# Moving two small tiles so that TensorE's two operands start a multiple of 512 bytes apart

## The chip, the cores and the metric

The kernel runs on one core of a Trainium2 chip. The metric is device time in microseconds of one execution, the median of several. The engines are named as the profile names them: PE is TensorE (its matmuls), PEld is TensorE's load of the stationary operand, DVE is VectorE, ACT is ScalarE, POOL is GpSimd, SP is SyncE, whose queue issues the weight transfers.

## The reference

One decoder block on 256 tokens of width 2048, all in float32. What is computed, cut to its matrix products:

```
x = x + 0.5 * swiglu(rmsnorm(x), w_gate, w_up, w_down)         # hidden width 5632
h = rmsnorm(x);  proj = h @ w_in                               # 2048 x 11264
y_a = diff_attention(dq, dk, dv);  y_b = hgrn2(hq, hf, hi, hg) # 8 heads each
merged = sigmoid(gate_a) * (y_a @ w_branch_a) + sigmoid(gate_b) * (y_b @ w_branch_b)
x = x + merged @ w_out
x = x + 0.5 * swiglu(rmsnorm(x), w_gate2, w_up2, w_down2)
x = x + sigmoid(rmsnorm(x) @ w_ple_gate) * rmsnorm(p @ w_ple_proj)
```

## The kernel before

All large products go through one stream of weights. A **group** is two blocks of 128 rows by 512 columns of a weight matrix. `prep` brings it from HBM into `raw` (SP's queue), rounds it to `wh` (ACT, line 114) and puts the remainder into `wl` (DVE, line 115), three groups ahead of use. `group` (lines 148 to 150) then multiplies: for each of the two blocks and each of the two halves of the tokens (`tt`) there are three matmuls, high activation by `wh`, high by `wl`, low by `wh`, so 12 matmuls in a group. The activation is the **stationary** operand, 128 by 128, loaded anew for every matmul; the weight is the **moving** operand, 128 by 512.

The activations stand in pairs of tiles, high and low part: `AH`, `AL` for the products of the normed block input (gate and up, `w_in`, `w_ple_gate`), `hH`, `hL` for the down products, `yaH`, `yaL` and `ybH`, `ybL` for the two branches, `mH`, `mL` for `w_out`, `pH`, `pL` for `w_ple_proj`. Of the 512-column matmuls 6672 load `AH` or `AL`, 2112 `hH` or `hL`, 384 `mH` or `mL`, 192 `ybH` or `ybL`, 192 `yaH` or `yaL`, 48 `pH` or `pL`.

The order of the work is written out by hand. Between two groups, `advance` lets each running task issue its next piece (transposes through PE, attention, the recurrence, residuals). A run of large matmuls is thus cut where a task puts small matmuls on PE: in the gate and up stage four transposes of `h` (line 209) after each 96 large matmuls, in the down stage four transposes of `x` at two places 12 matmuls apart in each chunk of 264, in the mixing stage at many places.

Where tiles stand: a pool lays its tags one behind the other, each buffer rounded up to 32 bytes, and a pool opened later stands behind those still open. Every weight buffer, `wh` and `wl` alike, starts 64 bytes above a multiple of 512. Inside the tiles a matmul's operand starts a multiple of 512 bytes from the tile's start (`AH[:, kt, tcol(tt)]` at 1024 kt + 512 tt, `wh[:, k2, :]` at 2048 k2). So the distance of the two operands, modulo 512, is that of the tiles:

```
tile         start (bytes in the partition)  start mod 512   minus that of wh, wl
wh, wl        93248 and on, steps of 4096         64              0
AH            34816                                0            -64
AL            51200                                0            -64
hH           126016                               64              0
hL           171072                               64              0
yaH, yaL     150592, 158784                       64              0
pH, pL       136256, 138304                       64              0
ybH, ybL     175200, 183392                       96            +32
mH, mL       191584, 207968                       96            +32
```

`AH` and `AL` follow `x` in the pool `base`; `ss4`, two buffers of 32 bytes, follows them. `gsub`, one number per partition (line 335), stands in the pool `mid` behind `yaL`, takes 32 bytes there, and so pushes all that the later pools put behind it, `ybH`, `ybL`, `mH` and `mL` among them, by 32 bytes.

## Time and profile before

| | |
|---|---|
| median of 3 runs | 2322.2 us (2322.05 to 2322.46) |
| profiled execution, first to last instruction | 2320.3 us |
| PE busy | 2312.7 us |
| DVE busy | 1270.9 us |
| ACT busy | 1042.7 us |
| HBM traffic | 186 GB/s over the span |

The profiled execution is told by its span alone; the median of the runs is 1.9 us longer, which is taken as what lies around the span. A matmul's row in the trace lasts longer than the step from one matmul to the next, since matmuls are pipelined: a row of 0.39 us stands beside a step of about 0.23 us. So the time that a matmul takes of the span is read from the starts of successive matmuls, not from its duration.

### The profile page before, as it was taken

How to read it: one execution, taken by the hardware profiler on the slowest of the kernel's cores; microseconds unless marked ns; L12 is line 12 of the kernel's file. 1: busy time of each engine (PE TensorE's matmuls, PEld its weight loads, DVE VectorE, ACT ScalarE, POOL GpSimd, SP SyncE). 2: the span in 40 equal slices, each digit the busy share in tenths (PEclk: the TensorE clock that was granted, in tenths of full speed). 3: DMA queues.
4: the chain of work that ended last, by engine and by line, in shares of the span. 5: the costliest groups of instructions: out<-in, count | busy, mean ns of one | idle time of the engine just before them, and what ended most of it. 6: DMA issues, size and time to landing. Idle time of an engine off the chain costs nothing.

```text
span 2320.3 us, 27206 instructions
## 1 busy us (share of the span) xinstructions
PE 2312.7 (100%) x10564; PEld 1903.2 (82%) x10564; DVE 1270.9 (55%) x1381; ACT 1042.7 (45%) x1270; POOL 39.5 (2%) x38
## 2 busy tenths in 40 slices
PE   9999999999999999999999999999999999999999
PEld 7888888888888888888888888888888888888887
DVE  5554555554444576667765555555555554444456
ACT  6444444444444455543344444544444444444454
POOL 0000000000000100000010000000000000000000
PEclk9999999999999999999999999999999999999999
DMA  8655555566666645554455655565555556666664
GB/s 292 190 182 191 190 188 185 189 189 188 188 188 196 201 161 167 186 173 153 160 156 181 186 186 181 179 193 184 189 190 185 188 188 190 193 188 191 188 213 149
DMA packets 120464, 432.55 MB, mean 186 GB/s; under 512 B 13773, under 2 KB 14181, under 8 KB 120208
## 3 DMA queue, kind: packets, MB, share of 16 engines
q1 hardware_dynamic: 118800, 426.33, 58.3%
q0 software_dynamic: 1248, 4.43, 0.5%
q8 instruction: 82, 1.34, 0.2%
q14 instruction: 46, 0.38, 0.0%
q10 hardware_dynamic: 288, 0.07, 0.0%
HBM read 428.67 MB, written 2.11 MB: 186 GB/s over the span
## 4 chain that ended last, share of the span: by engine, by line
PE 99%; DMA 1%; DVE 0%; ACT 0%; SPq 0%; issue 0%; ACTq 0%; DVEq 0%
PE acc L148 32%; PE acc L150 31%; PE acc L149 31%; PE tp L209 1%; PE ms L616 1%; DMA raw<-in_gu 0%; PE tp L219 0%; PE ms L440 0%; PE ms L150 0%; PE ms L149 0%; PE ms L148 0%; PE ms L589 0%; PE tp L362 0%; DMA junk<-in_xT 0%; PE tp L477 0%; PE ms L641 0%
## 5 line engine op out<-in xcount | busy, mean ns | idle before, releaser
L115 DVE TENSOR_TENSOR wl<-raw,wh 128x1024 fp32r<-128x1024 f32 (+1 forms) x805 | 983.9, 1223 | 888.9 <-ACT wh L114 886.5
L114 ACT CAST wh<-raw 128x1024 fp32r<-128x1024 f32 (+1 forms) x805 | 844.9, 1051 | 941.1 <-PE acc L150 915.6
L148 PE MATMUL acc<-wh,AH 128*128 128x512 f32 x2224 | 885.2, 398 | 0.2 <-ACT wh L114 0.2
L150 PE MATMUL acc<-wh,AL 128*128 128x512 f32 x2224 | 872.3, 392 | 0.0
L149 PE MATMUL acc<-wl,AH 128*128 128x512 f32 x2224 | 866.9, 390 | 1.6 <-DVE wl L115 1.6
L150 PEld LDWEIGHTS acc<-wh,AL 128*128 128x128 f32 x2224 | 417.7, 188 | 95.5
L149 PEld LDWEIGHTS acc<-wl,AH 128*128 128x128 f32 x2224 | 418.1, 188 | 91.5 <-DVE wl L115 3.7
L148 PEld LDWEIGHTS acc<-wh,AH 128*128 128x128 f32 x2224 | 418.4, 188 | 84.7 <-ACT wh L114 1.7
L148 PE MATMUL acc<-wh,hH 128*128 128x512 f32 x704 | 275.3, 391 | 0.0
L150 PE MATMUL acc<-wh,hL 128*128 128x512 f32 x704 | 274.2, 390 | 0.0
L149 PE MATMUL acc<-wl,hH 128*128 128x512 f32 x704 | 273.9, 389 | 0.0
L150 PEld LDWEIGHTS acc<-wh,hL 128*128 128x128 f32 x704 | 132.1, 188 | 27.8
L149 PEld LDWEIGHTS acc<-wl,hH 128*128 128x128 f32 x704 | 132.2, 188 | 27.1
L148 PEld LDWEIGHTS acc<-wh,hH 128*128 128x128 f32 x704 | 132.2, 188 | 27.1
L263 ACT ACTIVATE s<-acc,rowr 128x256 f32<-128x256 f32 x86 | 40.8, 477 | 49.9 <-PE acc L150 49.9
L183 ACT CAST hH<-tp 128x512 fp32r<-128x512 f32 x44 | 25.8, 587 | 74.7 <-PE tp L209 74.7
L184 DVE TENSOR_TENSOR hL<-tp,hH 128x512 fp32r<-128x512 f32 x44 | 30.4, 692 | 46.6 <-ACT hH L183 46.5
L265 DVE SCALAR_TENSOR_TENSOR h<-acc,rowr,s 128x256 f32<-128x256 f32 x86 | 41.4, 483 | 20.6 <-ACT s L263 20.6
L148 PE MATMUL acc<-wh,mH 128*128 128x512 f32 x128 | 51.3, 401 | 0.0
L149 PE MATMUL acc<-wl,mH 128*128 128x512 f32 x128 | 50.6, 395 | 0.0
L150 PE MATMUL acc<-wh,mL 128*128 128x512 f32 x128 | 50.6, 395 | 0.0
L186 ACT ACTIVATE AH<-tp,gains 128x256 fp32r<-128x256 f32 x48 | 22.9, 477 | 31.0 <-PE tp L209 16.9
(191 smaller groups left out, 1019.9 us busy)
## 6 DMA issues: line engine op xcount, KB each, us to landing
raw<-in_gu SPq DMA_DIRECT2D x351, 512.0 KB, 3.5
raw<-in_down SPq DMA_DIRECT2D x176, 512.0 KB, 3.8
raw<-in_w_in SPq DMA_DIRECT2D x176, 512.0 KB, 3.6
raw<-in_w_out SPq DMA_DIRECT2D x32, 512.0 KB, 3.7
raw<-in_w_pg SPq DMA_DIRECT2D x32, 512.0 KB, 4.3
raw<-in_w_a SPq DMA_DIRECT2D x16, 512.0 KB, 3.5
raw<-in_w_b SPq DMA_DIRECT2D x16, 512.0 KB, 3.5
junk<-in_xT SPq DMA_DIRECT2D x8, 256.0 KB, 4.2
```

The source lines that it names most:

```text
L114: nc.scalar.copy(wh[:, ks, :], raw[:, ks, :])
L115: nc.vector.tensor_tensor(wl[:, ks, :], raw[:, ks, :], wh[:, ks, :].bitcast(F32), op=ALU.subtract)
L148: nc.tensor.matmul(dst, hi, wh[:, k2, cols], start=(kt == 0), stop=False)
L149: nc.tensor.matmul(dst, hi, wl[:, k2, cols], start=False, stop=False)
L150: nc.tensor.matmul(dst, lo, wh[:, k2, cols], start=False, stop=(kt == last))
L183: nc.scalar.copy(H, src)
L184: nc.vector.tensor_tensor(L, src, H.bitcast(F32), op=ALU.subtract)
L186: nc.scalar.activation(H, src, AF.Copy, scale=gain)
L209: nc.tensor.transpose(tp[:, i, tcol(tt)], src_of(tt, kt + i), ident)
L263: nc.scalar.activation(s, acc[tt][:, :HALF], AF.Silu, scale=rs[0][:, tt : tt + 1])
L265: nc.vector.scalar_tensor_tensor(h[tt], acc[tt][:, HALF:], rs[0][:, tt : tt + 1], s, op0=ALU.mult, op1=ALU.mult)
L616: nc.tensor.matmul(lp[:, i, tt, :], km[:, i, tt, :], q4[:, i, tt, :], start=True, stop=True)
```

## The change

Three small edits move tiles. `gsub` becomes the fifth column of the tile of `small` in the pool `base`, whose 16 bytes grow to 20 within the same 32. `ss4` is allocated ahead of `AH` and `AL` instead of behind them. No instruction is added, removed or moved on any engine, and the waits stand as they did; the one instruction that writes `gsub`, and those that read it, name another tile. Comments taken out of the file are left out here.

```
-    small = T(base, [P, 4], "small")
+    smalls = T(base, [P, 5], "small")
+    small, gsub = smalls[:, 0:4], smalls[:, 4:5]
     ident = T(base, [P, P], "ident")
     x = T(base, [P, NT, D], "x")
+    ss4 = new_ss4()
     act = new_act()
-    ss4 = new_ss4()
...
     yaH = T(mp, [P, NH, SEQ], "yaH", F32R)
     yaL = T(mp, [P, NH, SEQ], "yaL", F32R)
-    gsub = T(mp, [P, 1], "gsub")
     nc.vector.tensor_scalar(gsub, small[:, S_SUB : S_SUB + 1], 1.0 - LAMBDA_INIT, None, op0=ALU.mult)
```

After it `AH` starts at 34880 and `AL` at 51264 (64 above a multiple of 512), `ybH` and `ybL` at 175168 and 183360, `mH` and `mL` at 191552 and 207936 (64 above as well). `wh`, `wl`, `hH`, `hL`, `yaH`, `yaL`, `pH` and `pL` stay. So all tiles of the table have a distance of 0 modulo 512 from the weights. Other tiles of the attention, the recurrence and the merge move 32 bytes down; the operands of their small matmuls keep their distance, but for the products with `V`, whose `A` and `off` move while `V` stays, and the transposes of `tok`, `ya` and `SG` against `ident`, which stays.

## Rows read from the trace of the kernel before

**Rows 1.** The page: span, PE's busy time, granted clock by slice, chain that ended last.

```profile
span 2320.3 us, 27206 instructions
...
PE 2312.7 (100%) x10564; PEld 1903.2 (82%) x10564; DVE 1270.9 (55%) x1381; ACT 1042.7 (45%) x1270; POOL 39.5 (2%) x38
...
PEclk9999999999999999999999999999999999999999
...
PE 99%; DMA 1%; DVE 0%; ACT 0%; SPq 0%; issue 0%; ACTq 0%; DVEq 0%
```

**Rows 2.** What PE waited for: total us, times, longest.

```profile
PE acc L149 <- DVE wl L115: 1.6, 3, 0.8
PE ms L290 <- DVE warm L287: 1.2, 1, 1.2
```

**Rows 3.** The longest wait of all engines, the same columns.

```profile
ACT wh L114 <- PE acc L150: 915.6, 554, 3.5
```

**Rows 4.** PE's groups by line: out<-moving,stationary, count, busy us, mean ns.

```profile
L149 PE MATMUL acc<-wl,AH 128*128 128x512 f32 x2224 | 866.9, 390 | 1.6 <-DVE wl L115 1.6
L149 PE MATMUL acc<-wl,hH 128*128 128x512 f32 x704 | 273.9, 389 | 0.0
L149 PE MATMUL acc<-wl,mH 128*128 128x512 f32 x128 | 50.6, 395 | 0.0
L209 PE MATMUL tp<-ident,h 128*128 128x128 f32 x176 | 26.3, 271 | 0.0
L209 PE MATMUL tp<-ident,x 128*128 128x128 f32 x96 | 14.4, 272 | 0.0
L149 PE MATMUL acc<-wl,pH 128*128 128x512 f32 x16 | 6.2, 389 | 0.0
```

**Rows 5.** Timeline (start, duration us): a run of 96 on `AH`, `AL` between transposes.

```profile
281.74 0.48 PE L148 MATMUL acc<-wh,AH 128*128 128x512 f32 x1
282.05 0.40 PE L149 MATMUL acc<-wl,AH 128*128 128x512 f32 x1
...
303.58 0.39 PE L150 MATMUL acc<-wh,AL 128*128 128x512 f32 x1
```

**Rows 6.** Timeline: the run of 48 on `ybH`, `ybL`, first and last.

```profile
1272.27 0.40 PE L148 MATMUL acc<-wh,ybH 128*128 128x512 f32 x1
...
1283.24 0.40 PE L150 MATMUL acc<-wh,ybL 128*128 128x512 f32 x1
```

**Rows 7.** Timeline: a run of 84 on `mH`, `mL` behind transposes.

```profile
1415.41 0.48 PE L148 MATMUL acc<-wh,mH 128*128 128x512 f32 x1
1415.72 0.40 PE L149 MATMUL acc<-wl,mH 128*128 128x512 f32 x1
...
1434.86 0.39 PE L150 MATMUL acc<-wh,mL 128*128 128x512 f32 x1
```

**Rows 8.** Timeline: `hH`, `hL`, 264 from 506.00, then 12 from 566.34.

```profile
506.00 0.48 PE L148 MATMUL acc<-wh,hH 128*128 128x512 f32 x1
...
534.01 0.39 PE L148 MATMUL acc<-wh,hH 128*128 128x512 f32 x1
...
565.75 0.40 PE L150 MATMUL acc<-wh,hL 128*128 128x512 f32 x1
...
566.34 0.48 PE L148 MATMUL acc<-wh,hH 128*128 128x512 f32 x1
...
568.97 0.40 PE L150 MATMUL acc<-wh,hL 128*128 128x512 f32 x1
```

**Rows 9.** Timeline: `pH`, `pL`, the second and the last of a run of 24.

```profile
2238.65 0.40 PE L149 MATMUL acc<-wl,pH 128*128 128x512 f32 x1
...
2243.64 0.39 PE L150 MATMUL acc<-wh,pL 128*128 128x512 f32 x1
```

**Rows 10.** Timeline: `yaH`, `yaL`, first and last of 24 behind products with `V`.

```profile
1200.30 0.48 PE L148 MATMUL acc<-wh,yaH 128*128 128x512 f32 x1
...
1205.61 0.39 PE L150 MATMUL acc<-wh,yaL 128*128 128x512 f32 x1
```

## The prediction, made before the result was known

> **What bounds the kernel now.** I read the page first, then PE's waits, then PE's groups, then the timeline inside single stages. [...] PE waits 2.8 us in the whole span [rows 2], while the longest wait of all is that of ACT for PE, 915.6 us, because ACT may not overwrite a weight buffer that PE still reads [rows 3]. So the only thing that can move the end is the step from one large matmul to the next, and any change of that step reaches the end undiminished: ACT and DVE have slack in every group, and the transfers are issued three groups ahead.

> The step itself is not the same everywhere. The durations of the rows in the groups only hint at it (389 and 390 ns on `AH`, `hH` and `pH`, 395 ns on `mH`) [rows 4]; it must be taken from starts. On `AH`, `AL` the 95 matmuls from 282.05 to 303.58 make 94 steps in 21.53 us, 229.0 ns each [rows 5]. On `ybH` 47 steps take 10.97 us, 233.4 ns [rows 6]; on `mH` the 82 steps from 1415.72 take 19.14 us, 233.4 ns [rows 7]. On `hH` the last 140 steps of a run, 534.01 to 565.75, take 31.74 us, 226.7 ns [rows 8]; on `pH` 22 steps take 4.99 us, 226.8 ns [rows 9]. These are the same instructions, 128 by 128 stationary and 128 by 512 moving, with moving tiles from the same `wh` and `wl`. Set beside the table of places they fall into three classes: distance 0 modulo 512 gives 226.7 ns, distance -64 gives 229.0, distance +32 gives 233.4. The stage isn't the cause: `pH` runs between products on `AH`, and `ybH` between products on `AH` too, with the same side work around them. Nor is the part of memory: `hL` covers 171072 to 216128, which holds `ybH` and most of `mH`, and runs at the fast step. Inside a tile the step doesn't change from one token half to the other, though these stand 512 bytes apart, so what counts repeats within 512 bytes.

> **The change part by part.** No instruction, wait or transfer is added, removed or moved, so nothing has to be hidden; `gsub` is still written once by DVE, off the chain. What changes is the distance: 0 for `AH`, `ybH` and `mH` and their low parts.

> First, the steady step. 6672 matmuls on `AH`, `AL` (2224 on each of three lines) [rows 4] go from 229.0 to 226.7: 6672 x 2.3 = 15.3 us. 192 on `ybH`, `ybL` go from 233.4 to 226.7: 1.3 us. 384 on `mH`, `mL` the same: 2.6 us. Sum 19.2 us. The 96 half-wide matmuls at the end on `AH` have no row at distance 0; at most the same 2.3 ns each, 0.2 us, left out. The 2352 matmuls already at distance 0 gain nothing.

> Second, the restart, which works against the change. After small matmuls on PE the steady step isn't there at once. On `AH` a run from 281.74 to 303.58 has 95 steps in 21.84 us; at 229.0 they would take 21.76, so the restart costs 0.09 us over the steady step [rows 5]. On `hH` the 11 steps from 566.34 to 568.97 take 2.63 us and would take 2.49 at 226.7: 0.14 us [rows 8]. The run from 506.00 to 565.75, which follows transposes of `h` as the runs on `AH` do, has 263 steps in 59.75 us against 59.62: 0.13 us [rows 8]. On `yaH`, behind products with `V`, 23 steps take 5.31 us against 5.21: 0.10 us [rows 10]. So the aligned pair settles later, and a restart costs 0.01 to 0.05 us more than on `AH`. The program has 118 restarts on `AH`: 42 behind four transposes of `h` (176 transposes are 44 blocks, two of them ahead of `hH`) [rows 4], 42 behind other transposes, 34 behind small products. At 0.04, 0.05 and 0.01 us more: 1.7 + 2.1 + 0.3 = 4.1 us. On `mH` there are 8; the 83 steps from 1415.41 take 19.45 us against 19.37, 0.08 us for the restart [rows 7], so 0.06 more each: 0.5 us. Sum 4.6 us.

> Net 19.2 - 4.6 = 14.6 us. Against the profiled execution: span 2320.3 - 14.6 = 2305.7 us; with the 1.9 us around it, 2307.6.

> Bounds. Best: the restart on `AH` gets no dearer (one run alone stands for restarts behind transposes of `h`): gain 19.2, time 2303. Worst within the mechanism: every restart on `AH` costs what the dearest row shows, 0.14 us instead of 0.09, and those on `mH` the 0.06 more (5.9 + 0.5 us), and `AH` settles 0.4 ns above 226.7 (2.7 us; an estimate from the 0.01 us to which the rows are rounded, on 22 steps): gain 10.1, time 2312. The small matmuls whose distance changes (products with `V`, transposes against `ident`) have nothing at another distance that is alike; transposes of `x` and `h` stand at distances 0 and 64 from `ident` and their groups' means are 272 and 271 ns [rows 4], so some 200 of them are 0.2 us either way.

> The next bound after PE is far: a group of 12 takes 2.72 us instead of 2.75, and ACT still waits for PE for hundreds of us [rows 3]. PE's 2.8 us of waits [rows 2] may grow by what PE gains ahead of its first weights, 0.2 us.

> [...]

> **The rivals.**

> The second operand's place isn't what slows `AH`; only `ybH` and `mH` gain. For it: `AH` and `AL` stand lowest of all, partly below 65536, where no fast tile stands, and -64 is a different case from +32. Against it: the high and low tiles of the down products lie spread over 88 KB and run at one step, so place alone has shown no effect but by the distance. Gain 1.3 + 2.6 - 0.5 = 3.4 us: 2318.8.

> Distance has no effect at all, as if each tile carried its step with it by some other property (who wrote it, and when). For it: each kind of tile has its own writer. Against it: `ybH` and `yaH` are made by the same function (`branch_input`), and 23 steps on `yaH` with a restart among them take 5.31 us, 230.9 ns each, less than the 233.4 of `ybH` without one [rows 6, 10]. Time 2322.2.

> Slower: the aligned pair fails to settle. The place is the gate and up stage, 44 runs of about 96 matmuls behind transposes. On `hH` a restart costs 0.05 us more than on `AH`, spread over 11 steps [rows 8]: some 231.3 ns each beside what both pay, above the 229.0 of `AH`; if the runs of 96 stayed there, 4224 matmuls would lose 2.3 ns each, 9.7 us, and the mixing stage's runs of 12 to 36 (2112 matmuls) as much each, 4.9 us, against 3.4 gained on `ybH` and `mH`: 2322.2 + 11 = 2333. It decides when settling takes longer than the gain of a run pays for: 0.04 to 0.05 us more a restart against 2.3 ns a step, so 17 to 22 matmuls. Against it: the last 140 steps of a run on `hH` stand at 226.7 [rows 8]. Runs of 12 are on the wrong side of that point already, and their loss is in the sum.

> **How the numbers follow.** The mechanism as summed: 0.83, its own range 2303 to 2312. Only `ybH` and `mH`: 0.06. No effect: 0.05. Slower: 0.06. I predict 2307.6. For 8 in 10 the range must hold nearly all of the first case, so it goes a little beyond its bounds, 2302 to 2313, where a second unknown adds to the first. The runs of before agree within 0.4 us of each other; 0.2%, 4.6 us, is about what a measurement can tell from no change. The first case is faster (below 2317.6), the second and third are the same, the fourth is slower: 0.83, 0.11, 0.06.

> **What would show it.** The steady step on `AH`, `mH` and `ybH` at 226.7 ns in the timeline, and that on `hH`, `yaH` and `pH` unchanged. The first ten or so steps behind transposes in the gate and up stage above 226.7, making some 0.13 us a restart instead of 0.09. One chunk of that stage, 96 large matmuls and four transposes, some 0.18 us shorter than now. PE's waits still below 4 us, and ACT's for PE a little shorter. The prediction is wrong if the step on `AH` stays at 229.0 (then a place below 65536 or the tile itself is the cause), if it settles at a fourth value, or if the runs of 96 never settle.

## The result and the profile after

The changed kernel takes 2307.17 us (median of 4 runs, 2306.70 to 2307.39) against 2322.26 us of before: 15.1 us less, a ratio of 0.9935 with a 95% interval of 0.9923 to 0.9947. The forecast was 2307.6. The profiled executions differ by a little more, 2320.3 to 2304.2 us; the spans of the four runs after go from 2304.2 to 2305.3, so about 1 us of the 16.1 is play between executions.

The page of the changed kernel, lines as in [rows 1]:

```profile
span 2304.2 us, 27206 instructions
...
PE 2296.5 (100%) x10564; PEld 1903.1 (83%) x10564; DVE 1270.9 (55%) x1381; ACT 1041.0 (45%) x1270; POOL 39.4 (2%) x38
...
PE 98%; DMA 1%; DVE 0%; ACT 0%; SPq 0%; issue 0%; ACTq 0%
```

The whole gain is on PE: its busy time falls by 16.2 us, while DVE's stays and ACT's falls by 1.7 us. The waits of the changed kernel, total us, times and longest, as in [rows 2, 3]:

```profile
PE ms L290 <- DVE warm L287: 1.2, 1, 1.2
PE acc L149 <- DVE wl L115: 1.0, 2, 0.8
PE acc L148 <- ACT wh L114: 0.5, 1, 0.5
...
ACT wh L114 <- PE acc L150: 904.6, 554, 3.5
```

PE waits 2.7 us in all, 0.1 less than before, and ACT waits 11 us less for PE: PE was the bound and still is. The step was read as ahead, from the starts of large matmuls in the changed kernel's timeline (start, duration in us):

```profile
277.96 0.48 PE L148 MATMUL acc<-wh,AH 128*128 128x512 f32 x1
278.28 0.39 PE L149 MATMUL acc<-wl,AH 128*128 128x512 f32 x1
...
299.60 0.39 PE L150 MATMUL acc<-wh,AL 128*128 128x512 f32 x1
...
300.18 0.48 PE L148 MATMUL acc<-wh,AH 128*128 128x512 f32 x1
...
321.85 0.39 PE L150 MATMUL acc<-wh,AL 128*128 128x512 f32 x1
...
322.43 0.48 PE L148 MATMUL acc<-wh,AH 128*128 128x512 f32 x1
...
560.63 0.48 PE L148 MATMUL acc<-wh,hH 128*128 128x512 f32 x1
...
563.26 0.40 PE L150 MATMUL acc<-wh,hL 128*128 128x512 f32 x1
...
1264.60 0.39 PE L148 MATMUL acc<-wh,ybH 128*128 128x512 f32 x1
...
1275.25 0.39 PE L150 MATMUL acc<-wh,ybL 128*128 128x512 f32 x1
...
1405.28 0.48 PE L148 MATMUL acc<-wh,mH 128*128 128x512 f32 x1
...
1424.23 0.40 PE L150 MATMUL acc<-wh,mL 128*128 128x512 f32 x1
```

The run of 48 on `ybH` makes 47 steps in 10.65 us, 226.6 ns each, where it had 233.4 [rows 6]. A run of 96 on `AH` makes its 95 steps in 21.64 us, the next in 21.67, where one took 21.84 [rows 5]; at 226.7 ns they would take 21.54, so the restart behind transposes now costs 0.10 us in one chunk and 0.13 in the next, by turns. The 83 steps on `mH` take 18.95 us instead of 19.45 [rows 7], 0.13 over 18.82. The restart on `hH` is what it was, 2.63 us for 11 steps [rows 8]. One chunk of the gate and up stage, from the first large matmul to that of the next, lasts 22.22 and 22.25 us by turns, where it lasted 22.43 (326.59 to 349.02): 0.21 and 0.18 us less, with a forecast of some 0.18.

### The profile page after: what moved, and what is told of

It is laid out like the page before. It is cut to its first block, busy times and chain, and to the rows that moved or that the text cites. A ratio compares the mean times of both kernels' runs of the same rounds, so it can differ in the third digit from the quotient of the medians.

```text
span 2304.2 us, 27206 instructions
## 1 busy us (share of the span) xinstructions
PE 2296.5 (100%) x10564; PEld 1903.1 (83%) x10564; DVE 1270.9 (55%) x1381; ACT 1041.0 (45%) x1270; POOL 39.4 (2%) x38
## 4 chain that ended last, share of the span: by engine, by line
PE 98%; DMA 1%; DVE 0%; ACT 0%; SPq 0%; issue 0%; ACTq 0%
PE acc L148 31%; PE acc L150 31%; PE acc L149 31%; PE tp L209 1%; PE ms L616 1%; DMA raw<-in_gu 1%; PE tp L219 0%; PE ms L440 0%; PE ms L149 0%; PE ms L150 0%; PE ms L148 0%; PE ms L589 0%; PE tp L362 0%; ACT wh L114 0%; PE tp L477 0%
```

## The experiments

In all tables a step is worked out from two starts in the timeline of one run of large matmuls, past its first 12 where a restart lies ahead of it, divided by the steps between. The kernel before, run beside each group of experiments, took 2321.7 to 2322.5 us (medians).

**The two parts alone.** `e1` moves `ss4` only, `e2` moves `gsub` only.

```
 e1:                                   e2:
-    act = new_act()                   -    small = T(base, [P, 4], "small")
     ss4 = new_ss4()                   +    smalls = T(base, [P, 5], "small")
+    act = new_act()                   +    small, gsub = smalls[:, 0:4], smalls[:, 4:5]
                                       -    gsub = T(mp, [P, 1], "gsub")
```

Expected: 

> Only the move of ss4, so AH and AL stand at distance 0 from the weights and ybH, mH stay at +32. By the sum of the prediction 15.3 us of steady step less 4.1 us of dearer restarts is gained: 2322.2 - 11.2 = 2311.0 us. The steady step on AH at 226.7 ns, on ybH and mH at 233.4 ns. Rival, that ybH and mH alone gain by the whole change: 2322.2 us here.

Expected: 

> Only the move of gsub, so ybH, ybL, mH and mL stand at distance 0 and AH, AL stay at -64. By the sum 1.3 + 2.6 us of steady step less 0.5 us of restarts is gained: 2322.2 - 3.4 = 2318.8 us. The steady step on AH at 229.0 ns, on ybH and mH at 226.7 ns. Rival, that the two moves only work together: 2322.2 us.

Measured: `e1` 2310.17 us, ratio 0.9950 (0.9936 to 0.9964); `e2` 2319.03 us, ratio 0.9986 (0.9977 to 0.9995). The timeline of `e1`, on `AH` and on `ybH`:

```profile
148.49 0.39 PE L148 MATMUL acc<-wh,AH 128*128 128x512 f32 x1
...
167.30 0.39 PE L150 MATMUL acc<-wh,AL 128*128 128x512 f32 x1
...
1299.48 0.39 PE L148 MATMUL acc<-wh,ybH 128*128 128x512 f32 x1
...
1310.44 0.40 PE L150 MATMUL acc<-wh,ybL 128*128 128x512 f32 x1
```

And that of `e2`:

```profile
149.27 0.39 PE L148 MATMUL acc<-wh,AH 128*128 128x512 f32 x1
...
168.26 0.39 PE L150 MATMUL acc<-wh,AL 128*128 128x512 f32 x1
...
1305.39 0.39 PE L148 MATMUL acc<-wh,ybH 128*128 128x512 f32 x1
...
1316.06 0.39 PE L150 MATMUL acc<-wh,ybL 128*128 128x512 f32 x1
```

In `e1` 83 steps on `AH` take 18.81 us, 226.6 ns, and 47 on `ybH` 10.96 us, 233.2 ns; in `e2` it is the other way round, 18.99 us, 228.8 ns, and 10.67 us, 227.0 ns. Each part speeds up the tiles that it puts in place and no other, and the gains of 12.1 and 3.3 us add up to 15.4, against 15.1 for both together.

**The distance, or a place.** `e3` shifts everything by 32 bytes.

```
+    T(base, [P, 8], "pad")
     gains = T(base, [P, 4, KD], "gains")
```

Expected: 

> The changed kernel with an unused tile of 32 bytes ahead of all others, so that every tile starts 96 instead of 64 bytes above a multiple of 512 and all distances stay 0. If the distance of the two operands counts, nothing changes: 2307.2 us and 226.7 ns on every kind of tile. Rival, that a place of 64 modulo 512 counts for a stationary tile by itself (96 was the slow place of ybH and mH, 233.4 ns): 9600 matmuls at 6.7 ns more, 2371 us.

Measured: 2307.70 us, ratio 0.9938 (0.9925 to 0.9952). The timeline of `e3`:

```profile
148.18 0.39 PE L148 MATMUL acc<-wh,AH 128*128 128x512 f32 x1
...
166.99 0.39 PE L150 MATMUL acc<-wh,AL 128*128 128x512 f32 x1
```

83 steps in 18.81 us, 226.6 ns, with every operand at the place modulo 512 where `ybH` had been slow. What counts is where the tiles stand to each other.

**Which distances.** `s1` and `s2` set unused tiles between the others, so that each pair of activation tiles stands at a distance of its own; `s4` shifts by a few bytes, by cutting a pair out of one tile that is 32 bytes longer; its distances are told modulo 256, the others modulo 512.

```
     act = new_act()                                   # s1: AH at 256
+    T(base, [P, 64], "pad_a")
...
+            T(fp, [P, 32], "pad_h")                   # s1: hH at 128
             hH = T(fp, [P, DFF // P, SEQ], "hH", F32R)
...
+        t = T(pool, [P, 2 * n + 8], tag, F32R)        # s4: pair, start o elements in
+        return tuple(t[:, o + i * n : o + (i + 1) * n].rearrange("p (k s) -> p k s", s=SEQ) for i in range(2))
```

Expected: 

> The changed kernel with unused tiles between the others, so that six distances stand beside each other in one run: AH, AL 256; hH, hL 128; yaH, yaL 64; ybH, ybL 192; mH, mL 320; pH, pL 384 bytes, modulo 512. If only a multiple of 512 is fast, as the words of the change have it, every kind of tile steps at 229 to 234 ns and the time is over that of the kernel before, 2322 to 2350 us. Rival, a shorter period: those at multiples of 128 or 256 step at 226.7 ns, and only yaH, ybH and mH are slower. [...]

Expected: 

> Six distances showed the same step at 0 and 256 (226.7 ns), at -64 and 192 (229.0), at 64 and 320 (233.4), so the period is 256. Here the three 32-byte places left in it, each on two kinds of tile: 160 on AH and ybH, 224 on hH and mH, 96 on yaH and pH. If the step falls with nearness to the next multiple from below (128: 232.6, 192: 229.0, 256: 226.7), 160 gives about 231 and 224 about 228 ns, and 96 about 233. Rival, that only multiples of 64 behave so and odd multiples of 32 stand on the wrong foot: 233.4 ns on all three, as at 32. Both kinds of tile at one distance must agree, else the distance isn't the whole cause.

Expected: 

> Distances of a few bytes, where the changed kernel has 0: AH, AL -16; hH, hL 16; yaH, yaL 8; ybH, ybL -8; mH, mL 4; pH, pL -4. If memory is read in lines of some 16 bytes or more, 4 and 8 bytes up stay at 226.7 ns, and 16 either way changes the step towards 228 (below 0) and 233 ns (above). Rival, that the distance counts byte by byte: 4 and 8 bytes give steps between those of 0 and 32. If AH at -16 is at or below 226.7 ns, the time is 2307 us or less.

Measured: `s1` 2322.82 us, ratio 1.0002 (0.9992 to 1.0012), the time of before; `s2` 2364.05 and `s4` 2316.09 us, one run each.

| kernel | tile | distance | first start | last start | steps | ns a step |
|---|---|---|---|---|---|---|
| s1 | `AH` | 256 | 148.96 | 167.77 | 83 | 226.6 |
| s1 | `hH` | 128 | 569.62 | 625.39 | 239 | 233.3 |
| s1 | `yaH` | 64 | 1209.95 | 1212.75 | 12 | 233.3 |
| s1 | `mH` | 320 | 1417.50 | 1434.06 | 71 | 233.2 |
| s1 | `ybH` | 192 | 1306.82 | 1317.36 | 46 | 229.1 |
| s1 | `pH` | 384 | 2239.13 | 2244.25 | 22 | 232.7 |
| s2 | `AH` | 160 (416) | 128.82 | 148.19 | 83 | 233.4 |
| s2 | `hH` | 224 | 582.27 | 638.03 | 239 | 233.3 |
| s2 | `yaH` | 96 | 1231.66 | 1234.47 | 12 | 234.2 |
| s2 | `ybH` | 160 | 1329.72 | 1340.69 | 47 | 233.4 |
| s2 | `mH` | 224 | 1419.14 | 1435.71 | 71 | 233.4 |
| s2 | `pH` | 96 | 2278.48 | 2283.87 | 23 | 234.3 |
| s4 | `AH`, one run | -16 | 149.12 | 168.07 | 83 | 228.3 |
| s4 | `hH`, one run | 16 | 571.11 | 625.28 | 239 | 226.7 |
| s4 | `yaH` | 8 | 1206.24 | 1209.01 | 12 | 230.8 |
| s4 | `ybH` | -8 | 1303.02 | 1313.76 | 46 | 233.5 |
| s4 | `mH` | 4 | 1414.29 | 1430.80 | 71 | 232.5 |
| s4 | `pH` | -4 | 2232.79 | 2237.77 | 22 | 226.4 |

Three of the rows of `s1`, word for word from its timeline:

```profile
148.96 0.39 PE L148 MATMUL acc<-wh,AH 128*128 128x512 f32 x1
...
167.77 0.39 PE L150 MATMUL acc<-wh,AL 128*128 128x512 f32 x1
...
1417.50 0.39 PE L148 MATMUL acc<-wh,mH 128*128 128x512 f32 x1
...
1434.06 0.40 PE L150 MATMUL acc<-wh,mL 128*128 128x512 f32 x1
```

256 is as good as 0 (226.6 ns on `AH` here and in `e3`), 192 is as -64 was (229.1 and 228.9), 320 as 64 (233.2 and 233.3): the relation repeats every 256 bytes, not every 512, and the words of the change ask for more than is needed. (At 384, which is 128, `pH` steps at 232.4 to 232.7 ns; `hH` at 128 stands at 233.3 in the second run of each down stage, which is the one in the table, and at 232.4 in the others, where a pattern of seven unequal steps repeats.) The slope that I expected for `s2` fell: 160 and 224 are as slow as 32 (233.3 and 233.4 ns, against 233.2 on `ybH` in `e1`), on both kinds of tile each. So did the reading in lines of 16 bytes: 4 and 8 bytes already cost 4 to 6 ns. And the distance isn't all: `AH` at -16 steps at 228.3 ns in every second chunk and at 226.7 in those between, `hH` at 16 at 233.3 in the first run of its stage and at 226.7 in the others. The timeline of `s4`, for a chunk between the slow ones of `AH` (83 steps in 18.82 us) and for the first run on `hH` (251 steps in 58.56 us):

```profile
126.88 0.39 PE L148 MATMUL acc<-wh,AH 128*128 128x512 f32 x1
...
145.70 0.40 PE L150 MATMUL acc<-wh,AH 128*128 128x512 f32 x1
...
505.97 0.40 PE L148 MATMUL acc<-wh,hH 128*128 128x512 f32 x1
...
564.53 0.39 PE L150 MATMUL acc<-wh,hH 128*128 128x512 f32 x1
```

The chunks of `AH` also write to two pairs of output buffers by turns, so there the buffer could be what differs; most of the first run on `hH` and most of the third write to the same pair and step at 233.3 and 226.7, so there it isn't.

**Which pair of operands.** While one matmul runs, the stationary tile of the next is loaded: in the changed kernel the load for line 150 (PEld) begins with the matmul of line 149 and is done after 0.19 us, before the matmul of line 150 begins.

```profile
289.85 0.39 PE L149 MATMUL acc<-wl,AH 128*128 128x512 f32 x1
289.85 0.19 PEld L150 LDWEIGHTS acc<-wh,AL 128*128 128x128 f32 x1
290.08 0.39 PE L150 MATMUL acc<-wh,AL 128*128 128x512 f32 x1
```

`p1`, `p2` and `p3` put the low activation tiles, `wl`, or both 64 bytes off, so that the pair in one matmul and the pair at work at the same time differ.

```
         wh = T(wp, [P, 2, NB], "wh", F32R)
+        if n == 0:
+            T(wp, [P, 16], "pad_w", bufs=1)           # p1 and p3
         wl = T(wp, [P, 2, NB], "wl", F32R)
...
+        T(base, [P, 16], "pad_al")                    # p1 and p2, and so for hL, yaL, ybL, mL, pL
         lo = T(base, [P, KD, SEQ], "AL", F32R)
```

Expected: 

> In the changed kernel wl and all low activation tiles (AL, hL, yaL, ybL, mL, pL) move 64 bytes up against wh and the high tiles. A matmul's own operands then stand at 0 (wh, high), -64 (wl, high) and +64 (wh, low). But while a matmul's moving tile streams, the stationary tile of the next one is loaded, and those pairs all stand at distance 0: wh with the high tile, wl with the low one, wh with the high one. If the load of the next stationary tile against the running stream is what counts: step 226.7 ns, about 2307 us. Rival, the own operands count: steps of 226.7, 229.0 and 233.4 ns, 229.7 in the mean, 9648 matmuls at 3.0 ns more, 2336 us.

Expected: 

> As the kernel p1, but wl stays with wh and only the low activation tiles move 64 bytes up. Both readings now have one pair of three at +64: the load of the low tile under the stream of wl, or the low tile with its own wh. Both give (226.7 + 226.7 + 233.4) / 3 = 228.9 ns, 9600 matmuls at 2.2 ns more less some 2 us of cheaper restarts: 2326 us. If the first reading holds, the step behind line 149 is the longer one, if the second, the step behind line 150. Were it a matter of the low tiles' own place, p1 would be as slow as this.

Expected: 

> The changed kernel with wl alone 64 bytes up against wh; all activation tiles, high and low, at distance 0 from wh. p1 and p2 both came out at a mean step of 231.1 ns, though in p1 each load stood at distance 0 from the stream under it; in both, the stationary tile jumps by 64 bytes from the high to the low tile and back. If jumps from one stationary tile to the next are what costs there: here there are none, one pair of three stands at -64, and the step is at most the 228.9 ns of the old AH, 2307 to 2328 us. If any jump between successive matmuls costs, that of the moving tile too: 231.1 ns again, 2343 us.

Measured: `p1` 2343.39 us, ratio 1.0090 (1.0075 to 1.0105); `p2` 2342.56, ratio 1.0085 (1.0069 to 1.0102); `p3` 2352.23, ratio 1.0132 (1.0116 to 1.0147). The timeline of `p1`, in which lines 150 to 152 are the three matmuls:

```profile
577.02 0.40 PE L150 MATMUL acc<-wh,hH 128*128 128x512 f32 x1
...
632.26 0.39 PE L152 MATMUL acc<-wh,hL 128*128 128x512 f32 x1
```

239 steps in 55.24 us, 231.1 ns; in `p2` the same run takes 55.23 us (577.15 to 632.38), in `p3` 83 steps on `AH` take 19.26 us (129.17 to 148.43), 232.0 ns. Both readings fell: the loads of `p1` all stand at 0 to the stream under them and yet it is slow; by a matmul's own pair it should be at 229.7. The steps line by line, means over the first run on `hH` behind its first 12 matmuls, say so too. In `p2` the steps behind the three matmuls are 228.3, 229.1 and 235.9 ns: the long one is behind the third, where the second reading had put it. In `p1` they are 232.6, 231.7 and 229.1, and here the second reading had put the longest behind the third and the shortest behind the first, the reverse of what came. That jumps of the stationary tile cost fell with `p3`, which has none and is the slowest. What the three show is weaker: it isn't enough that one kind of pair is in place; with the low tile, with `wl` or with both 64 bytes off, the steps behind all three matmuls are longer in the mean than 226.7 ns (231.5 to 232.3 in `p3`, where single steps go from 224 to 241), also those whose own operands stand at 0. `wh` and the high tile weren't moved alone.

**The way through memory.** `x1` stores tokens by turns, so that a stationary operand is read with a stride.

```
-                hi, lo = AH[:, kt, tcol(tt)], AL[:, kt, tcol(tt)]
+                if "AH" in str(AH.name):
+                    hi, lo = (mixed(t[:, kt, :])[:, tt, :] for t in act)      # "p (j t) -> p t j"
+                elif "hH" in str(AH.name):
+                    hi, lo = (mixed2(t[:, kt - k2 : kt - k2 + 2, :])[:, k2, tt, :] for t in act)
```

Expected: 

> The changed kernel with the tokens in AH, AL stored in turn from the two token tiles, so that a stationary operand is read with a stride of 2 elements (128 columns over 1024 bytes), and in hH, hL with a stride of 4 (over 2048 bytes, as many as the moving operand); the other tiles as they were. ACT and DVE write those tiles with that stride. [...]

Measured: 2370.71 us, ratio 1.0212 (1.0195 to 1.0229). The loads of `x1` (count, busy us, mean ns), whose lines 159 and 160 are the first two matmuls:

```profile
L159 PEld LDWEIGHTS acc<-wh,AH 128*128 128x128 f32 x2224 | 432.2, 194 | 85.9 <-ACT wh L114 1.9 <-ACT AH L197 0.6
...
L160 PEld LDWEIGHTS acc<-wl,hH 128*128 128x128 f32 x704 | 220.2, 313 | 0.0
```

83 steps on `AH` take 19.37 us (130.27 to 149.64), 233.4 ns, and `hH` stands at 235.0 (239 steps from 585.58 to 641.74) in the first two runs of its stage and at 236.7 in the others. The rows of the load go from 188 ns to 194 with a stride of 2 and to 313 with 4, longer than the step itself. So a strided load doesn't shorten the step here. But the test doesn't tell whether the stride is what made it longer: by the turn of the tokens half of the operands in `AH` start 4 bytes off a multiple of 256, and those in `hH` 0, 4, 8 or 12, and a few bytes alone cost 4 to 7 ns on some tiles of `s4`.

**A better place than 0?** `c1` puts all activation tiles 4 bytes below a multiple of 256, `c2` puts the same tiles back on it.

```
-    def pair(pool, k, tag, o=7):
+    def pair(pool, k, tag, o=8):
```

Expected: 

> The changed kernel with all activation tiles 4 bytes below a multiple of 256 from the weights instead of on it; H and L of a pair are cut from one tile for that. pH, pL at -4 stepped at 226.6 ns in the run of a few bytes, the only distance besides 0 and 256 that settled there alone, and AH at -16 had restarts of 0.09 to 0.11 us over the steady step against 0.10 to 0.13 at distance 0. If -4 keeps the step of 0 and restarts as cheaply as that: some 150 restarts at 0.03 us less, 4 us, 2303 us, a version better than the changed kernel. Rival, restarts as at 0, or runs that settle at a slower step as some did at -16: 2307 us or more.

Expected: 

> The kernel before this one, c1, with its pairs of tiles 4 bytes higher and nothing else changed, so that all activation tiles stand on a multiple of 256 bytes from the weights again. c1 stepped at 233.3 ns on every kind of tile and took 2364 us, though pH, pL had stepped at 226.6 at the same distance of -4. If the 4 bytes are what made c1 slow: 226.7 ns and 2307 us here. Rival, that the cut of H and L from one tile made it slow: 2364 us again.

Measured: `c1` 2364.25 us, ratio 1.0180 (1.0166 to 1.0194); `c2` 2307.38 us, ratio 0.9938 (0.9922 to 0.9955). Four bytes cost 56.9 us. The timeline of `c2` on `AH`, 83 steps in 18.81 us:

```profile
147.87 0.39 PE L148 MATMUL acc<-wh,AH 128*128 128x512 f32 x1
...
166.68 0.39 PE L150 MATMUL acc<-wh,AH 128*128 128x512 f32 x1
```

The timeline of `c1` on `AH` and on `pH`:

```profile
128.66 0.40 PE L148 MATMUL acc<-wh,AH 128*128 128x512 f32 x1
...
148.03 0.39 PE L150 MATMUL acc<-wh,AH 128*128 128x512 f32 x1
...
2278.94 0.40 PE L149 MATMUL acc<-wl,pH 128*128 128x512 f32 x1
...
2284.07 0.40 PE L150 MATMUL acc<-wh,pH 128*128 128x512 f32 x1
```

And that of `s4`, where `pH` stands at the same -4:

```profile
2232.79 0.39 PE L149 MATMUL acc<-wl,pH 128*128 128x512 f32 x1
...
2237.77 0.39 PE L150 MATMUL acc<-wh,pH 128*128 128x512 f32 x1
```

In `c1` 83 steps on `AH` take 19.37 us, 233.4 ns, and 22 on `pH` 5.13 us, 233.2; in `s4` the 22 take 4.98 us, 226.4. (In both the low tile bears the name of its pair.) The same distance, two steps: in `s4` the run on `pH` follows one on `AH` at -16 without small matmuls between, in `c1` one on `AH` at -4. At this distance a run keeps, it seems, the rhythm in which it is entered; from a restart `c1` never gets into the fast one. At others it doesn't: `ybH` at -8 in `s4` steps at 233.3 in all four runs, which follow `AH` at 226.7 as well as at 228.4. No place was found that beats 0.

## Why the prediction was right

**The bound.** PE's step was named as the only thing that can move the end. PE's busy time and the span fell by the same 16 us, and every kernel here moved as its steps did.

**The steady step.** Forecast 226.7 ns on `AH`, `ybH` and `mH`, unchanged elsewhere; measured 226.6 on `ybH`, 226.7 on `AH` (83 steps from 147.36 to 166.18, 18.82 us). `e1` and `e2` show that each part acts on its own tiles alone, `e3` that it is the distance; `c1` and `c2`, which differ by 4 bytes in the place of the stationary tiles, step at 233.4 and 226.6 ns on `AH`. That is the part of the cause that is shown: the same instructions at the same places in the program, with nothing moved but tiles.

**The restart.** Forecast 0.13 us a restart in the gate and up stage and 0.14 on `mH`; measured 0.10 and 0.13 by turns, and 0.13. All starts of both traces, each restart taken over the settled step of its run, tell more. The 118 restarts on `AH` cost 0.098 us each in the mean before and 0.124 after, so 3.1 us more and not 4.1: 0.020 more behind transposes of `h` and 0.024 behind other transposes (forecast 0.04 and 0.05), but 0.036 behind small products (forecast 0.01, from the one kind of row on `yaH`). With 0.4 us on `mH` the term is 3.5 us where the sum has 4.6.

The steady term was too large as well. The 229.0 ns on `AH` were read from the second matmul of a run on, with steps of the restart among them; past the first 12 the step is 228.9 (83 steps in 19.00 us, 127.59 to 146.59). At 228.89 against 226.67 the 6672 matmuls give 14.8 us, and the term is 18.7 us, not 19.2. So the net by measured sizes is 15.2 us, close to the 15.1 that the runs show; the forecast of 14.6 missed it by little because two errors, 0.5 us up and 1.1 us down, partly cancelled, and that part is luck. Without the restarts the sum would have been 2303, 4 us too low: it was worth reading what a restart of the aligned pair costs where it already ran.

**The rivals.** That only `ybH` and `mH` gain fell with `e1`; that distance has no effect, with all three of `e1`, `e2` and `e3`. That the aligned pair never settles, with the run from 277.96. What a pair that doesn't settle in the fast step costs is seen at another distance: in `c1`, at -4, none does, and the kernel is 42 us slower than before.

**What was wrong.** I said that what counts repeats within 512 bytes, which is true, but 256 is the period. I read the three classes as a property of the distance; `s4` and `c1` show two steps at one distance, so something else counts too, most likely the state in which a run begins, which no run varied alone. I took it that the aligned pair settles later; in the changed kernel the run on `AH` from 277.96 is at 227 ns from the fifth step on and that from 300.18 only from the eleventh, and in `c2`, at the same distance, every chunk restarts in the slower way (22.25 us each). And I took a reading in pairs for granted in the experiments `p1` to `p3`, which none of the pairs explains. Two readings of no weight were off as well: the range of `hL` holds all of `mH`, not most of it, and the 2112 matmuls of the mixing stage on `AH` stand in runs of up to 120, not of 12 to 36 alone.

**Open.** What in the chip makes the step 226.7, 229 or 233 ns isn't shown; `p1`, at 231.1 ns on `hH` with every load at 0 to the stream beside it, shows that the distance of one load to the one stream beside it isn't the whole of it. Why neighbouring chunks restart differently isn't known.

## What to carry to other kernels

When PE is busy to the end and all matmuls have one shape, compare the step, start to start, between stages: a stage that steps 1 to 3% slower than another with the same instructions (here 228.9 and 233.3 ns against 226.7) may owe it to where its tiles stand, and the fast stage tells what the gain would be. Then, for matmuls of this shape and type, put stationary tiles, high and low, and moving tiles all on a multiple of 256 bytes from each other, exactly, and read the step again, since a few bytes can be worse than 64 (on `AH` 233.4 ns at -4 in `c1`, 228.9 at -64 before). Count the restarts too: here a restart on `AH` became 0.026 us dearer in the mean and a step 2.2 ns shorter, so a run must be some 12 matmuls long (an estimate from these two) before the better step pays.

## What the runs showed of the hardware that was not expected

| distance (kernel) | steps in the pattern | ns the pattern lasts | times 6.67 ns | ns a step |
|---|---|---|---|---|
| 0, 256 | 1 | 226.7 | 34 | 226.7 |
| -64 (before), 192 (s1) | 3 | 686.7 | 103 | 228.9 |
| -16 (s4, every second chunk) | 4 | 913.3 | 137 | 228.3 |
| 8 (s4) | 5 | 1153.4 | 173 | 230.7 |
| low tile 64 off (p2), low tile and `wl` (p1) | 3 | 693.3 | 104 | 231.1 |
| `wl` 64 off (p3) | 15 | 3480.0 | 522 | 232.0 |
| 128 (s1, most runs), 4 (s4) | 7 | 1626.7 | 244 | 232.4 |
| -8 (s4), -4 (c1) | 1 | 233.3 | 35 | 233.3 |
| 32 (before), 64 and 320 (s1) | 2 | 466.7 | 70 | 233.3 |
| 160 (s2) | 3 | 700.0 | 105 | 233.3 |
| 224 (s2) | 4 | 933.3 | 140 | 233.3 |

Nothing settled below 226.7 (226.4 and 226.6 ns in the tables above are 226.7 within the 0.01 us of the starts).

Distances of 4 to 16 bytes behave in no order: -8 gives 233.5 ns, 8 gives 230.8, 4 gives 232.5, 16 gives 233.3 or 226.7, and -4 gave 226.4 in one kernel and 233.2 in another.

The row of a load lasts 188 ns; with the stationary operand read with a stride of 2 elements it lasts 194, with a stride of 4 it lasts 313 (`x1`).
